# Pinning the block sums of feed-forward tile pairs in VectorE's program order

## The chip, the cores and the metric

The kernel runs on one core of one Trainium2 chip. The metric is the device time of one launch in microseconds (us). The core's engines run side by side, each through a queue of its own in a fixed order: TensorE (PE, with its weight loads shown as PEld), VectorE (DVE), ScalarE (ACT), GpSimd (POOL) and SyncE (SP), which here issues nearly all transfers between on-chip memory and DRAM. An engine that waits at an instruction holds up everything behind it in its queue.

## The reference

One layer of a transformer trunk on 1024 tokens with 1024 features: an attention mixer, then a feed-forward (SwiGLU), each with a modulated input and a layer norm on the way out. The change touches the feed-forward alone:

```python
def swiglu(h, w_in, w_out):                 # h 1024x1024, w_in 1024x5632, w_out 2816x1024
    gate, up = jnp.split(h @ w_in, 2, axis=-1)
    return (jax.nn.silu(gate) * up) @ w_out
...
x = layer_norm(DEEPNORM_ALPHA * x + gate2 * swiglu(h, ffn_w_in[i], ffn_w_out[i]), ln_g[i, 1], ln_b[i, 1])
```

All values are float32; the kernel splits each operand into a high and a low part and adds three products.

## The kernel before, in words

**The first products.** The hidden width of 2816 is cut into 22 feed-forward tiles of 128 (`ff`). For each, the products of the input with the gate and up weights are formed by a scheme of seven block products (a Strassen-Winograd form) rather than eight. They are the steps 1, 6, 2, 7, 5, 4, 3 of a tile, and a step is 12 matmuls (four blocks of the contraction by three partial products, lines 1073 to 1075). Steps 1 and 2 of the tiles 0 to 5 run ahead of the rest, so these tiles have five steps each (6, 7, 5, 4, 3: 60 matmuls); from tile 6 (`FIRST`) on all seven steps stand in a row (84 matmuls).

**The banks.** Steps 1 and 2 write PSUM banks `A`, of which there are two. Steps 6, 7 and 4 add up in one bank `B`, and steps 5 and 3 in one bank `D`, and there is one of each. After every step VectorE reads the bank as it then stands, and only when it has read it may the next step on that bank start: after step 6 line 1086 (`u2 = B + p1`), after 7 line 1088 (`u3 = B + p1`), after 5 line 1090 (`ub = D + u3`), after 4 line 1093 (`ua = B + p1`), after 3 line 1097 (`gb = D + u2`). TensorE can go on meanwhile with another bank. In tiles 0 to 5 step 7 follows step 6 on the same bank; the scheduler puts the first four or five matmuls of step 5 (bank `D`) between them as cover. From tile 6 on all of step 2 (bank `A`) lies there.

**The hidden tiles.** After step 3, ScalarE takes the silu of `gb` (line 1098) and GpSimd multiplies it in (`ub = ub * gb`, line 1099); `ua` has its own product on GpSimd after step 4 (line 1094). `u2` has one place in the tile `fd`, so that line 1086 of the next tile must stand behind line 1097 of this one. `ua` and `ub` have two places, for even and odd tiles.

**The block sums of a pair.** The second products, with `w_out`, use the same seven-product form, and want sums of the hidden blocks of two neighbouring tiles. `hidden_sums` makes them, four sums a pair, 11 pairs: `hs1 = ub + vb` (line 991), `hs2 = hs1 - ua` (992), `hs3 = ua - ub` (995), `hs4 = va - hs2` (996), where `ua`, `ub` are of the even tile and `va`, `vb` of the odd one. Each is stored to DRAM by SyncE (`store_hidden`, line 982). In the program's text the sums are written two steps after step 3 of the odd tile (lines 991 and 992) and one step later again (lines 995 and 996), through the list `late`.

**Other work beside it.** For each coming step one weight block is split: ScalarE casts the high part (line 844), VectorE subtracts for the low part (line 845); eight steps' blocks are held in `slots`. GpSimd makes the weight blocks' own sums (lines 828 to 831). The weight tiles `wi` are loaded two tiles ahead (line 804). Every ten steps `out_weights` makes sums of the `w_out` weights on VectorE (lines 1009 to 1013), already pinned.

**What sets the order.** The program is traced line by line and a scheduler then orders each engine's queue by its own estimate of when operands are ready; an instruction that it takes to be ready early moves ahead. `keep` is `tc.keep_in_program_order`: it ties an instruction behind the one that was traced just before it on the same engine. It adds no wait for another engine.

**After the first products.** The second products load their operands (`r`, lines 870 to 875) from the stored sums and the stored weights (`td`), split them as `ring` (lines 1029 and 1030), and multiply (lines 1222 to 1224). The two rows loaded at line 1143 reuse the memory of the block sums, so SyncE waits there for their stores.

Of the kernel before, what the change touches and what calls it, by code (L numbers as in the profile page):

```python
# [12 lines left out]
ALU = mybir.AluOpType  # L13
# [32 lines left out]
def fox_trunk_kernel(  # L46
# [17 lines left out]
    nc = tc.nc  # L64
# [911 lines left out]
    keep = tc.keep_in_program_order  # L976
# [4 lines left out]
    def store_hidden(ff, t, i):  # L981
        nc.sync.dma_start(sd[i][ff // 2], t)

    hs = {}

    def hidden_sums(ff, k, ua, ub, va, vb):

        if k == 0:
            hs.update({n: fp.tile([P, 512], F32, name=f"hs{n}_{ff}", tag=t, **({"bufs": 2} if t == "hb0" else {}))
                       for n, t in ((1, "a0"), (2, "a1"), (3, "hb0"), (4, "hb0"))})  # L990
            nc.vector.tensor_tensor(hs[1], ub, vb, ALU.add)
            nc.vector.tensor_tensor(hs[2], hs[1], ua, ALU.subtract)
            done = (5, hs[1]), (6, hs[2])
        else:
            nc.vector.tensor_tensor(hs[3], ua, ub, ALU.subtract)
            nc.vector.tensor_tensor(hs[4], va, hs[2], ALU.subtract)
            done = (7, hs[3]), (3, hs[4])
        for i, t in done:
            store_hidden(ff, t, i)
# [58 lines left out]
    def step(n):  # L1058
# [22 lines left out]
        if i == 1:  # L1081
            nc.scalar.copy(p1, b)
        elif i == 2:
            nc.scalar.activation(sa, b, AF.Silu)
        elif i == 6:
            nc.vector.tensor_tensor(u2, b, p1, ALU.add)  # L1086
        elif i == 7:
            nc.vector.tensor_tensor(u3, b, p1, ALU.add)
        elif i == 5:
            nc.vector.tensor_tensor(ub, b, u3, ALU.add)  # L1090
        elif i == 4:

            nc.vector.tensor_tensor(ua, b, p1, ALU.add)
            nc.gpsimd.tensor_tensor(ua, ua, sa, ALU.mult)
            late.append((n + 2, lambda: store_hidden(ff, ua, 1 + ff % 2)))
        else:
            nc.vector.tensor_tensor(gb, b, u2, ALU.add)
            nc.scalar.activation(gb, gb, AF.Silu)
            nc.gpsimd.tensor_tensor(ub, ub, gb, ALU.mult)
            if ff % 2:  # L1100
                late.append((n + 2, lambda: store_hidden(ff, ub, 4)))
                for k in range(2):
                    late.append((n + 2 + k + (ff + 1 >= FIRST), lambda k=k: hidden_sums(ff, k, fd[:, 4], fd[:, 2], fd[:, 5], fd[:, 3])))
# [200 lines left out]
```

## Time and profile before

| | us |
|---|---|
| median of 3 runs | 1428.95 (1426.27 to 1428.96) |
| profiled execution | 1424.15 |
| its span, first to last instruction | 1422.4 |
| PE busy | 1354.8 |
| DVE busy | 1011.5 |
| ACT busy | 585.2 |
| POOL busy | 340.1 |

The mean granted TensorE clock of the profiled execution is 0.989 of full speed. The first products run from about 762 to 1200 us of the span, the second ones from there to the end.

In the rows below a line of a timeline is: start in us, length in us, engine, source line, operation, tiles written and read, count; in brackets how long the engine had been idle and what released it. Lengths of one engine's instructions overlap a little, so the distance of starts is the better measure of a sequence. A line of the windows view is: stretch, its length, busy time (and instructions) of PE, PEld, DVE, ACT and POOL, the granted clock, the busy share of the transfer engines, GB/s. A line of the waits view is: who waited for whom, total us, times, longest.

### The profile page before, as it was taken

The page shows a single profiled execution, that of the slowest core. Times are in us where ns is not written, and L with a number is a line of the kernel's source. Part 1 is how long each engine was busy: PE and PEld are TensorE (multiplying, and loading weights), DVE is VectorE, ACT ScalarE, POOL GpSimd, SP SyncE. Part 2 cuts the span into 40 slices and gives each one's busy share as a digit, 9 for nine tenths or more (in the row PEclk, how much of TensorE's full clock was granted, in tenths as well). Part 3 has the DMA queues.
Part 4 walks back from the last instruction along what each step waited for, and adds up shares of the span by engine and source line. Part 5 has one row for each costly group of instructions (what it writes and reads, how often), then busy time and mean ns, then how long its engine had stood idle before and what let it go on. Part 6 is the DMA issues. An engine that isn't in the chain of part 4 may idle for free.

```text
span 1422.4 us, 19155 instructions
## 1 busy us (share of the span) xinstructions
PE 1354.8 (95%) x6832; PEld 1134.3 (80%) x6832; DVE 1011.5 (71%) x1636; ACT 585.2 (41%) x1025; POOL 340.1 (24%) x250
## 2 busy tenths in 40 slices
PE   5899999999999999999999889999999999899997
PEld 4677778887888888889997667888888888688886
DVE  6765586655988888888767655566666667685897
ACT  3532232123777776784236322333333334543320
POOL 2443003310111111132000444444444431000011
PEclk9999999999999999999999999999999999999999
DMA  9757775568655566527444332554655566996631
GB/s 274 202 175 235 245 215 182 186 192 213 143 130 138 135 151 151 137 82 258 165 147 137 96 119 95 195 175 158 199 191 167 181 205 228 348 296 225 193 119 74
DMA packets 212305, 254.41 MB, mean 179 GB/s; under 512 B 13353, under 2 KB 138609, under 8 KB 212210
## 3 DMA queue, kind: packets, MB, share of 16 engines
q1 hardware_dynamic: 211058, 251.09, 58.4%
q10 hardware_dynamic: 1152, 2.10, 0.4%
q8 instruction: 54, 0.88, 0.3%
q14 instruction: 41, 0.34, 0.1%
HBM read 185.18 MB, written 67.96 MB: 178 GB/s over the span
## 4 chain that ended last, share of the span: by engine, by line
PE 70%; DVE 12%; DMA 5%; POOL 5%; issue 4%; ACT 2%; SPq 1%; POOLq 0%; DVEq 0%; ACTq 0%
PE og L631 5%; PE y L1222 4%; PE y L1223 4%; PE y L1224 4%; PE B L1073 4%; PE t L596 4%; PE B L1075 4%; PE B L1074 4%; PE A L1073 3%; PE A L1074 3%; PE A L1075 3%; PE D L1075 3%; PE D L1074 2%; PE D L1073 2%; PE s L535 2%
## 5 line engine op out<-in xcount | busy, mean ns | idle before, releaser
L1222 PE MATMUL y<-ring 128*128 128x512 f32 (+1 forms) x319 | 122.7, 385 | 5.2 <-ACT fpu L1181 5.2
L1029 ACT CAST ring<-r 128x1024 fp32r<-128x1024 f32 x77 | 80.5, 1055 | 105.9 <-PE y L1224 59.1
L1030 DVE TENSOR_TENSOR ring<-r,ring 128x1024 fp32r<-128x1024 f32 x77 | 95.4, 1249 | 38.9 <-ACT ring L1029 31.0
L1223 PE MATMUL y<-ring 128*128 128x512 f32 (+1 forms) x319 | 122.6, 384 | 0.0
L1224 PE MATMUL y<-ring 128*128 128x512 f32 (+1 forms) x319 | 122.2, 384 | 0.0
L1073 PE MATMUL B<-XT,slots 128*128 128x512 f32 x264 | 105.0, 398 | 15.7 <-DVE fd L1086 12.7
L602 DVE TENSOR_TENSOR pl<-t,ph 128x512 fp32r<-128x512 f32 x192 | 103.9, 549 | 14.8 <-ACT ph L601 13.5
L844 ACT CAST slots<-wi 128x512 fp32r<-128x512 f32 x88 | 54.4, 623 | 141.7 <-PE D L1074 69.3
L543 ACT ACTIVATE p<-s,nm 128x640 f32<-128x640 f32 (+7 forms) x128 | 95.5, 746 | 39.1 <-DVE nm L542 38.7
L601 ACT CAST ph<-t 128x512 fp32r<-128x512 f32 x192 | 91.1, 480 | 44.3 <-PE t L596 41.8
L1074 PE MATMUL B<-XT,slots 128*128 128x512 f32 x264 | 103.7, 393 | 0.0
L1075 PE MATMUL B<-XT,slots 128*128 128x512 f32 x264 | 103.7, 393 | 0.0
L542 DVE TENSOR_REDUCE nm<-s 128x1 f32<-128x640 f32 (+7 forms) x128 | 95.6, 749 | 2.5
L596 PE MATMUL t<-ident,p 128*128 128x128 f32 x576 | 95.7, 273 | 0.6 <-DVE pl L602 0.4
L596 PEld LDWEIGHTS t<-ident,p 128*128 128x128 f32 x576 | 71.3, 141 | 11.5 <-DVE pl L602 2.2
L845 DVE TENSOR_TENSOR slots<-wi,slots 128x512 fp32r<-128x512 f32 x88 | 70.8, 804 | 9.8 <-ACT slots L844 9.8
L579 PE MATMUL o<-ph,va 128*128 128x512 f32 x192 | 76.5, 399 | 0.0
L1222 PEld LDWEIGHTS y<-ring 128*128 128x128 f32 x319 | 60.3, 189 | 18.5 <-ACT fpu L1181 5.6
L1073 PEld LDWEIGHTS B<-XT,slots 128*128 128x128 f32 x264 | 50.3, 191 | 29.2 <-DVE fd L1086 15.2
L535 PE MATMUL s<-ka,qa 128*128 128x320 f32 (+2 forms) x192 | 67.5, 352 | 5.0 <-ACT p L543 4.9
L1224 PEld LDWEIGHTS y<-ring 128*128 128x128 f32 x319 | 60.4, 189 | 11.8
L1223 PEld LDWEIGHTS y<-ring 128*128 128x128 f32 x319 | 60.4, 189 | 11.6
(571 smaller groups left out, 3747.1 us busy)
## 6 DMA issues: line engine op xcount, KB each, us to landing
wi<-in_ffn_w_in_dram SPq DMA_DIRECT2D x50, 512.0 KB
aw<-in_ada_w_dram SPq DMA_DIRECT2D x46, 512.0 KB
r<-sd SPq DMA_DIRECT2D x77, 256.0 KB
sd<-hs SPq DMA_DIRECT2D x44, 256.0 KB
r<-td SPq DMA_DIRECT2D x44, 256.0 KB
sd<-fd SPq DMA_DIRECT2D x33, 256.0 KB
r<-in_ffn_w_out_dram SPq DMA_DIRECT2D x33, 256.0 KB
qa<-qs SPq DMA_DIRECT2D x32, 256.0 KB
```

The costliest lines, as they stand in the source:

```text
L535: nc.tensor.matmul(o, qa[:, q], ka[:, c0:c0 + w], start=True, stop=False)
L542: nc.vector.tensor_reduce(nm, view, axis=axis, op=ALU.max, negate=True)
L543: nc.scalar.activation(pv, view, AF.Exp, bias=nm, accum_out=lcs[hf][:, s * 4 + jj:s * 4 + jj + 1])
L596: nc.tensor.transpose(tb[:, jj * P:(jj + 1) * P], probs[hf * 4 + jj][:, kbk * P:(kbk + 1) * P], ident)
L602: nc.vector.tensor_tensor(pl[:, c0:], tb[:, c0:], f32(ph[:, c0:]), ALU.subtract)
L1030: nc.vector.tensor_tensor(t[:, 1], raw, f32(t[:, 0]), ALU.subtract)
L1073: nc.tensor.matmul(b, hi, rh, start=(first and k == 0), stop=False, skip_group_check=True)
L1074: nc.tensor.matmul(b, hi, rl, start=False, stop=False, skip_group_check=True)
L1075: nc.tensor.matmul(b, lo, rh, start=False, stop=(k == 3), skip_group_check=True)
L1222: nc.tensor.matmul(b[:, c0:c1], sh, wh, start=first, stop=False, skip_group_check=True)
L1223: nc.tensor.matmul(b[:, c0:c1], sh, wl, start=False, stop=False, skip_group_check=True)
L1224: nc.tensor.matmul(b[:, c0:c1], sl, wh, start=False, stop=last, skip_group_check=True)
```

## The change

The four block sums are each wrapped in `keep`, and nothing else is altered:

```diff
         if k == 0:
...
-            nc.vector.tensor_tensor(hs[1], ub, vb, ALU.add)
-            nc.vector.tensor_tensor(hs[2], hs[1], ua, ALU.subtract)
+            keep(nc.vector.tensor_tensor(hs[1], ub, vb, ALU.add))
+            keep(nc.vector.tensor_tensor(hs[2], hs[1], ua, ALU.subtract))
             done = (5, hs[1]), (6, hs[2])
         else:
-            nc.vector.tensor_tensor(hs[3], ua, ub, ALU.subtract)
-            nc.vector.tensor_tensor(hs[4], va, hs[2], ALU.subtract)
+            keep(nc.vector.tensor_tensor(hs[3], ua, ub, ALU.subtract))
+            keep(nc.vector.tensor_tensor(hs[4], va, hs[2], ALU.subtract))
             done = (7, hs[3]), (3, hs[4])
```

The same instructions run on every engine; their order differs on VectorE and SyncE, a little on TensorE and ScalarE, and not on GpSimd. In the rows below `hs_1` are the sums of the pair of tiles 0 and 1 (the number at the end tells the four apart), `hs_7` of tiles 6 and 7, `hs_21` of 20 and 21; the numbers behind `B` and `D` tell the tiles apart.

VectorE where tile 0 ends and tile 1 begins, the difference:

```order
 L1097 TENSOR_TENSOR fd<-D_8666,fd 128x512
 L845 TENSOR_TENSOR slots<-sqb,slots 128x512
-L995 TENSOR_TENSOR hs_1_8840<-fd 128x512
 L1086 TENSOR_TENSOR fd<-B_8719,fc 128x512
 L845 TENSOR_TENSOR slots<-wi_12_8543,slots 128x512
```

`hs3` needs the even tile alone, and stood ahead of line 1086 of tile 1; it is gone from there. The same holds after tiles 2 and 4.

VectorE where tile 1 ends and tile 2 begins, before:

```order
L1097 TENSOR_TENSOR fd<-D_8755,fd 128x512
L845 TENSOR_TENSOR slots<-sqb,slots 128x512
L991 TENSOR_TENSOR hs_1_8838<-fd 128x512
L1086 TENSOR_TENSOR fd<-B_8808,fc 128x512
L845 TENSOR_TENSOR slots<-wi_14_8664,slots 128x512
L992 TENSOR_TENSOR hs_1_8839<-hs_1_8838,fd 128x512
L996 TENSOR_TENSOR hs_1_8841<-fd,hs_1_8839 128x512
L1088 TENSOR_TENSOR fd<-B_8808,fc 128x512
L845 TENSOR_TENSOR slots<-skb,slots 128x512
L1090 TENSOR_TENSOR fd<-D_8853,fd 128x512
```

and now:

```order
L1097 TENSOR_TENSOR fd<-D_8755,fd 128x512
L845 TENSOR_TENSOR slots<-sqb,slots 128x512
L1086 TENSOR_TENSOR fd<-B_8808,fc 128x512
L845 TENSOR_TENSOR slots<-wi_14_8664,slots 128x512
L991 TENSOR_TENSOR hs_1_8838<-fd 128x512
L992 TENSOR_TENSOR hs_1_8839<-hs_1_8838,fd 128x512
L1088 TENSOR_TENSOR fd<-B_8808,fc 128x512
L845 TENSOR_TENSOR slots<-skb,slots 128x512
L995 TENSOR_TENSOR hs_1_8840<-fd 128x512
L996 TENSOR_TENSOR hs_1_8841<-fd,hs_1_8839 128x512
L1090 TENSOR_TENSOR fd<-D_8853,fd 128x512
```

Line 1086 now stands ahead of all four sums; two of them stand ahead of line 1088 and two ahead of line 1090. The boundary after tile 3 reads the same.

VectorE after line 1086 of tile 8, where the sums of tiles 6 and 7 now meet the pinned sums of the `w_out` weights:

```order
L1086 TENSOR_TENSOR fd<-B_9470,fc 128x512
L845 TENSOR_TENSOR slots<-wi_25_9300,slots 128x512
L991 TENSOR_TENSOR hs_7_9499<-fd 128x512
L992 TENSOR_TENSOR hs_7_9500<-hs_7_9499,fd 128x512
L845 TENSOR_TENSOR slots<-sqb,slots 128x512
L1009 TENSOR_TENSOR gate1b<-gate1b 128x512
L1010 TENSOR_TENSOR gate1b<-gate2b,gate1b 128x512
L995 TENSOR_TENSOR hs_7_9501<-fd 128x512
L996 TENSOR_TENSOR hs_7_9502<-fd,hs_7_9500 128x512
L1088 TENSOR_TENSOR fd<-B_9470,fc 128x512
```

Before, all four stood ahead of line 1086 here. The sums of tiles 16 and 17 stand the same way; the other pairs from tile 4 on have no weight sums between lines 1086 and 1088, but for tiles 12 and 13, where they stand ahead of line 991.

SyncE, the stores of the last pair and the first loads behind them, before:

```order
L982 DMA sd_10_7028<-hs_21_11330 128x512
L982 DMA sd_10_7039<-hs_21_11331 128x512
L1237 DMA gate2b<-g2d 128x1024
L982 DMA sd_10_7006<-hs_21_11333 128x512
L870 DMA r_14_11377<-sd_3_7032 128x512
L875 DMA r_14_11377<-td_7054 128x512
L870 DMA r_15_11394<-sd_4_7033 128x512
L1143 DMA ln_11353<-in_ln_g_dram 128x1024
```

and now:

```order
L982 DMA sd_10_7028<-hs_21_11330 128x512
L982 DMA sd_10_7039<-hs_21_11331 128x512
L982 DMA sd_10_7050<-hs_21_11332 128x512
L982 DMA sd_10_7006<-hs_21_11333 128x512
L1237 DMA gate2b<-g2d 128x1024
L870 DMA r_14_11377<-sd_3_7032 128x512
L1143 DMA ln_11353<-in_ln_g_dram 128x1024
L1143 DMA ln_11355<-in_ln_b_dram 128x1024
L875 DMA r_14_11377<-td_7054 128x512
L870 DMA r_15_11394<-sd_4_7033 128x512
```

The store of `hs3` (sd_10_7050), which was issued some twenty rows earlier, is now among the last four, and two loads of `r` moved behind line 1143.

On TensorE step 5 lies around step 7: at each of the first four boundaries (into tiles 1 to 4) five of its matmuls stood ahead of step 7 and seven behind it, and now four and eight, as the boundary into tile 5 had it already.

## Rows read from the trace of the kernel before

**Rows 1.** The page, part 1: busy time, share, instructions of each engine.

```profile
PE 1354.8 (95%) x6832; PEld 1134.3 (80%) x6832; DVE 1011.5 (71%) x1636; ACT 585.2 (41%) x1025; POOL 340.1 (24%) x250
```

**Rows 2.** Windows view of a late stretch of the first products.

```profile
1150.00:1200.00 50.00, 50.00 (x222) 41.20 (x221) 33.67 (x44) 19.67 (x27) 12.29 (x9) 1.00 0.64 218
```

**Rows 3.** Waits view of PE, 760 to 1240 us.

```profile
PE B L1073 <- DVE fd L1086: 12.7, 6, 2.7
PE y L1222 <- ACT fpu L1181: 5.2, 1, 5.2
PE B L1073 <- DVE fd L1088: 3.0, 1, 3.0
```

**Rows 4.** Timeline of DVE, from tile 0 to tile 1 of the feed-forward.

```profile
808.27 0.69 DVE L1097 TENSOR_TENSOR fd<-D,fd 128x512 f32<-128x512 f32 x1 [1.43 <-PE D L1075]
...
812.43 1.73 DVE L995 TENSOR_TENSOR hs<-fd 128x512 f32<-128x512 f32 x1 [2.64 <-POOL fd L1099]
814.09 0.68 DVE L1086 TENSOR_TENSOR fd<-B,fc 128x512 f32<-128x512 f32 x1
814.69 1.15 DVE L845 TENSOR_TENSOR slots<-wi,slots 128x512 fp32r<-128x512 f32 x1
```

**Rows 5.** Timeline of POOL in the same stretch.

```profile
811.11 1.29 POOL L1099 TENSOR_TENSOR fd<-fd 128x512 f32<-128x512 f32 x1
812.35 1.26 POOL L830 TENSOR_TENSOR wi<-sqb,wi 128x512 f32<-128x512 f32 x1
```

**Rows 6.** Timeline of DVE: a step of tile 1, then tile 4 to 5.

```profile
820.89 0.69 DVE L1090 TENSOR_TENSOR fd<-D,fd 128x512 f32<-128x512 f32 x1 [0.31 <-PE D L1075]
...
823.61 0.69 DVE L1093 TENSOR_TENSOR fd<-B,fc 128x512 f32<-128x512 f32 x1 [1.43 <-PE B L1075]
...
877.55 0.69 DVE L1097 TENSOR_TENSOR fd<-D,fd 128x512 f32<-128x512 f32 x1 [1.43 <-PE D L1075]
...
880.32 0.69 DVE L995 TENSOR_TENSOR hs<-fd 128x512 f32<-128x512 f32 x1 [1.47 <-POOL fd L1099]
880.93 0.68 DVE L1086 TENSOR_TENSOR fd<-B,gate2b 128x512 f32<-128x512 f32 x1
...
891.97 0.69 DVE L1097 TENSOR_TENSOR fd<-D,fd 128x512 f32<-128x512 f32 x1 [0.97 <-PE D L1075]
```

**Rows 7.** Timeline of PE at the two boundaries of rows 4 and 6.

```profile
811.70 0.39 PE L1074 MATMUL D<-XT,slots 128*128 128x512 f32 x1
814.82 0.80 PE L1073 MATMUL B<-XT,slots 128*128 128x512 f32 x1 [2.73 <-DVE fd L1086]
...
880.75 0.39 PE L1073 MATMUL D<-XT,slots 128*128 128x512 f32 x1
881.67 0.50 PE L1073 MATMUL B<-XT,slots 128*128 128x512 f32 x1 [0.53 <-DVE fd L1086]
882.00 0.39 PE L1074 MATMUL B<-XT,slots 128*128 128x512 f32 x1
```

**Rows 8.** Windows view of two single microseconds of the first products.

```profile
816.00:817.00 1.00, 1.00 (x4) 0.81 (x3) 0.00 (x0) 0.00 (x0) 0.00 (x0) 0.50 0.26 47
...
867.00:868.00 1.00, 1.00 (x3) 0.73 (x3) 0.97 (x3) 0.00 (x0) 0.00 (x0) 0.50 0.04 12
```

**Rows 9.** Timeline of DVE, after tile 7 of the feed-forward.

```profile
938.70 0.70 DVE L845 TENSOR_TENSOR slots<-sqb,slots 128x512 fp32r<-128x512 f32 x1 [1.85 <-ACT slots L844]
...
941.61 0.68 DVE L1088 TENSOR_TENSOR fd<-B,fc 128x512 f32<-128x512 f32 x1
...
949.09 0.69 DVE L1097 TENSOR_TENSOR fd<-D,fd 128x512 f32<-128x512 f32 x1 [0.50 <-PE D L1075]
```

**Rows 10.** Timeline of DVE, block sums of the last pair.

```profile
1207.13 0.68 DVE L992 TENSOR_TENSOR hs<-hs,fd 128x512 f32<-128x512 f32 x1
...
1208.87 0.68 DVE L996 TENSOR_TENSOR hs<-fd,hs 128x512 f32<-128x512 f32 x1
```

**Rows 11.** Windows view of the load-bound stretch between first and second products.

```profile
1210.00:1215.00 5.00, 5.00 (x24) 4.14 (x23) 0.68 (x1) 0.00 (x0) 0.00 (x0) 1.00 0.90 273
```

## The prediction

> **What bounds the kernel now.** I read from the whole to the place. The page's first part has TensorE busy for 95% of the span and VectorE for 71% [rows 1], so an edit on VectorE is worth only what TensorE waits for it. In the first products from tile 6 on TensorE does not wait at all: 50.00 us busy in 50 us, 222 matmuls [rows 2]. The waits view of TensorE for the whole stage has three lines: 12.7 us for line 1086 in six waits, 3.0 us for line 1088 in one, and 5.2 us in one wait for a ScalarE copy, where the second products begin [rows 3]. The prize is in the first line. The place is the boundary from one tile to the next in tiles 0 to 5, seen in VectorE's timeline: line 1097 at 808.27, then a sum (line 995) which stands idle for 2.64 us and takes 1.73 us, and only then, at 814.09, line 1086 [rows 4]. The sum waits for GpSimd's product of line 1099, which ends at 811.11 + 1.29 = 812.40 [rows 5]. Line 1086 needs no part of it; it is only queued behind it.
>
> **What is lost there now.** Twelve matmuls take 2.72 us where nothing waits (line 1090 at 820.89 to line 1093 at 823.61) [rows 6], so one takes 0.227 and the 60 of a tile 13.60. From line 1097 of tile 0 at 808.27 [rows 4] to that of tile 5 at 891.97 [rows 6] there are five tiles in 83.70 us, where 5 x 13.60 = 68.00 would do: 15.70 us lost. The parts: at the first boundary the matmul after 811.70 could start at 811.93 and starts at 814.82, a gap of 2.89; the next matmul after a gap also comes 0.33 instead of 0.227 later (881.67 to 882.00), 0.10 more [rows 7]. Four boundaries are alike, 4 x 2.99 = 11.96. The fifth, from 877.55 to 891.97, loses 14.42 - 13.60 = 0.82 [rows 6]. That makes 12.78. [...]
>
> [...]
>
> **The change, part by part.** It adds no wait and no instruction. It moves 44 sums on VectorE with the SyncE stores that hang on them; GpSimd's queue stays as it is.
>
> *Line 1086 goes free.* At every boundary its earliest start is then step 6's end, 2.72 after line 1097: 880.27 at the fifth one, where it started at 880.93 behind a sum [rows 6]. TensorE follows 0.74 later (881.67 for 880.93), so at 881.01. The four matmuls of cover end with the one at 880.75, so the slot is 880.98 [rows 7]. That leaves 0.03 + 0.10 = 0.13 at each of five boundaries, since the first four now have four matmuls of cover too: **0.65 us stay**.
>
> *Two sums ahead of line 1088 (after tiles 1 and 3).* Counted from line 1097: line 1086 at 2.72, line 845 at 3.32, and if it takes 1.15 as in rows 4, line 991 at 4.47. Its GpSimd product is done at 812.40 - 808.27 = 4.13 [rows 4, 5], so the wait itself is hidden by lines 1086 and 845. Line 1088 must start by 7.22, so that step 4 has its slot at 3.43 + 20 x 0.227 = 7.96. No row shows the sums there; the neighbours are 0.69 [rows 6] and 1.73 [rows 4]. Two of 0.69 put line 1088 at 5.85, one of each at 6.89, two of 1.73 at 7.93, which is 0.71 + 0.10 too late, twice: 0 to 1.6. I take **0**, as one of each is still in time, and GpSimd's work of this kind ends soon after.
>
> The 1.73 stand beside GpSimd's line 830, which runs from 812.35 to 813.61 [rows 5]; the sum ends 0.55 after that, about its own 0.69. [...]
>
> *Two sums ahead of line 1090 (same places).* Line 1090 then starts at about 6.89 + 0.60 + 0.60 + 2 x 0.69 = 9.47; step 3 wants its bank at 7.96 + 2.72, so line 1090 may start as late as 9.94. Nothing is lost; this is the cover that is used up most.
>
> *Four sums ahead of line 1088 from tile 6 on.* There line 1088 may start 2 x 2.72 after line 1086, and since step 5 stands between, up to 7.22 after it without a wait. Six instructions at about 0.61 fit. Where the weight sums stand there too (pairs 6/7 and 16/17), lines 991 and 992 fall into VectorE's idle 1.85 us before 938.70, but lines 995 and 996 push line 1088 from 941.61 by 2 x 0.61 to 942.83. Line 1097 at 949.09 ran as soon as its bank was done [rows 9]; two steps before, 943.65, step 5 was done, the next step's slot is 0.20 before that (880.27 against 880.98 - 4 x 0.227 = 880.07 in rows 6, 7), and minus 0.74 the limit is 942.71. Late by 0.12 + 0.10, twice: **0.4 us lost**; none at best, and with one of the two sums at 1.73 some 2 x 1.34 = 2.7.
>
> *The last pair's stores.* TensorE already waits 5.2 us at the start of the second products [rows 3], for loads behind these stores in SyncE's queue. Before, line 996 starts 1.74 after line 992 (1207.13, 1208.87), with a split of `ring` between them; now line 995 is between, 2 x 0.60 = 1.20, so the last store is ready 0.54 earlier [rows 10]. But the store of `hs3`, 256 KB, comes into this stretch; at 273 GB/s with the transfer engines 0.90 busy [rows 11] it takes 0.96: 0.4 us net. Two loads of 256 KB moved behind line 1143's wait, up to 1.9 more. Ends: -0.5 if the store finds free time, 2.3 if nothing does. I count one of the two loads: **1.4 us lost**. The earlier pairs' stores move by some microseconds against weight loads that are two tiles ahead: nothing.
>
> **The sum.** 15.70 - 0.65 - 0 - 0.4 - 1.4 = 13.25 us. Nothing behind tile 5 waits for a clock of its own but the transfers above, so an earlier start is handed on to the end. The profiled execution took 1424.15 (span 1422.4 and 1.75 around it) and would take 1410.9. It was faster than all three timed runs; against their median of 1428.95 the sum gives **1415.7 us**.
>
> **The rivals.**
> (a) *The wait moves to line 1088.* If line 1099 comes later than in rows 5, line 991 waits as before and line 1088 is late in its place. That can be only after tiles 1 and 3: 2 x 2.99 come back, 13.25 - 6.0 = 7.3, **1421.7**. Against it speak the 0.34 us and the 1.37 of further cover (5.85 against 7.22).
> (b) *Given back at the second products.* If the loads there keep their time on the clock, the wait of 5.2 grows by all that was gained, and the kernel stays at **1428.9**. For it: the stretch is 0.90 busy with transfers [rows 11]. Against it: shortly before they are at 0.64 [rows 2], and most loads are issued when a buffer comes free, so they move along.
> (c) [...] If GpSimd runs beside the sums everywhere, each takes 1.73 and line 845 1.15. Then line 1088 starts 0.60 + 2 x 1.15 + 4 x 1.73 = 9.82 after line 1086 against 7.22: 2.60 + 0.10 for each of eight pairs (4/5 to 18/19) is 21.6, with 2.4 for the weight sums of two and 1.6 after tiles 1 and 3 it is 25.6; less the gain, 25.6 + 0.65 + 1.4 - 15.7 = 12.0 slower, **1440.9**. It decides at (7.22 - 0.60 - 2 x 0.69) / 4 = 1.31 us a sum. Against it: the sum of rows 6 takes 0.69. [...]
>
> **How the numbers follow.** Forecast 0.80, (a) 0.08, (b) 0.07, (c) 0.05. A measurement of this kernel can tell about 0.2%, 2.9 us, from no change. Faster: the forecast and (a), 0.88; within: (b), 0.07; slower: (c), 0.05. Range: at best 15.70 + 0.5, and two more slow-clock stretches saved in a usual run, 2.9, is 19.1: 1410. At worst 15.70 - 0.65 - 1.6 - 2.7 - 2.3, and one slow stretch left after the 3.0 us wait for line 1088, which the change does not touch, 1.46: 7.0, so 1422. (b) and (c) stay outside.
>
> **What would show it.** Right: the waits for line 1086 fall from 12.7 to under 2.5 us, of which 12.7 - 4 x 2.73 - 0.53 = 1.2 [rows 3, 7] belong to a wait inside tile 0 that stays; five tiles from line 1097 to line 1097 take 68 to 69 us; from tile 6 on TensorE stays at 50 in 50. Wrong: a new line for 1088 or 1090 in the waits of TensorE (a, c), or a wait for ScalarE's copy well above 6.6 (b).

## The result, and the profile after

The changed kernel takes **1408.83 us** (median of 4 runs, 1407.90 to 1410.20) against 1428.49 us (4 runs, 1426.27 to 1428.96) for the kernel before: a ratio of 0.9887, 95% interval 0.9860 to 0.9915. It is faster, as forecast, but by 19.7 us where 13.25 were predicted, and 1408.8 lies 1.2 us under the lower end of the range. The two profiled executions stand closer together: 1424.15 us before (span 1422.4) and 1409.46 us after (span 1407.7), 14.7 us apart. Compared again with more runs of the kernel before, the gain was 15.95 us (the second run of the changed kernel, below); the four runs of the kernel before here lie at the slow end of what it showed later, 1416.3 to 1428.3 us in 48 runs.

The waits view of TensorE covers the whole stage, 760 to 1240 us of the changed kernel (what waited, for whom; us in total, how often, the longest):

```profile
PE B L1073 <- DVE fd L1088: 4.8, 3, 3.1
PE y L1222 <- ACT fpu L1181: 2.8, 1, 2.8
PE B L1073 <- DVE fd L1086: 1.2, 1, 1.2
```

Against [rows 3], line 1086 has fallen from 12.7 us in six waits to the 1.2 us that belong to tile 0. Line 1088 has grown from one wait to three; the two new ones are 0.52 and 1.19 us. The wait at the start of the second products has fallen too, from 5.2 to 2.8 us, which I had not expected.

The starts of line 1097 in VectorE's timeline, one per tile, give the length of each tile (start, us, engine, line, operation; in brackets the idle time before it and who ended that):

```profile
808.02 0.69 DVE L1097 TENSOR_TENSOR fd<-D,fd 128x512 f32<-128x512 f32 x1 [1.43 <-PE D L1075]
...
821.80 0.69 DVE L1097 TENSOR_TENSOR fd<-D,fd 128x512 f32<-128x512 f32 x1 [1.43 <-PE D L1075]
...
836.36 0.69 DVE L1097 TENSOR_TENSOR fd<-D,fd 128x512 f32<-128x512 f32 x1 [1.43 <-PE D L1075]
```

Tile 1, from line 1097 of tile 0 to that of tile 1, takes 13.78 us and tile 2 takes 14.56. The next three, by the same line, take 13.78, 15.22 and 13.80; the five together 71.14 us instead of 83.70 [rows 4, 6]. The odd boundaries (after tiles 1 and 3) are the long ones. This is the first of them on VectorE:

```profile
824.52 0.69 DVE L1086 TENSOR_TENSOR fd<-B,fc 128x512 f32<-128x512 f32 x1 [1.20 <-PE B L1075]
825.12 1.35 DVE L845 TENSOR_TENSOR slots<-wi,slots 128x512 fp32r<-128x512 f32 x1
826.40 1.78 DVE L991 TENSOR_TENSOR hs<-fd 128x512 f32<-128x512 f32 x1
828.22 1.67 DVE L992 TENSOR_TENSOR hs<-hs,fd 128x512 f32<-128x512 f32 x1
829.81 0.68 DVE L1088 TENSOR_TENSOR fd<-B,fc 128x512 f32<-128x512 f32 x1
```

On GpSimd at that time, and then on TensorE:

```profile
825.88 1.75 POOL L830 TENSOR_TENSOR wi<-sqb,wi 128x512 f32<-128x512 f32 x1
827.71 1.62 POOL L831 TENSOR_TENSOR skb<-wi,wi 128x512 f32<-128x512 f32 x1
```

```profile
829.72 0.39 PE L1075 MATMUL D<-XT,slots 128*128 128x512 f32 x1
830.63 0.47 PE L1073 MATMUL B<-XT,slots 128*128 128x512 f32 x1 [0.52 <-DVE fd L1088]
```

Line 1086 is in time, 824.52, 2.72 us behind line 1097 as the prediction says. But both sums meet a GpSimd operation, line 830 and then line 831, and the two take 1.78 and 1.67 us instead of the 0.69 of [rows 6]. So line 1088 starts 8.01 us after line 1097, past the limit of 7.22, and TensorE's next matmul starts 0.91 after its predecessor instead of 0.23.

From tile 6 on TensorE does not wait, as before. The windows view of the changed kernel, columns as in [rows 2]:

```profile
900.00:950.00 50.00, 50.00 (x221) 41.13 (x220) 31.35 (x42) 15.49 (x27) 22.02 (x15) 1.00 0.52 174
1150.00:1200.00 50.00, 50.00 (x222) 41.20 (x221) 36.56 (x43) 19.84 (x24) 6.96 (x5) 1.00 0.75 253
```

VectorE has more to do there all the same. In the whole kernel it is busy for 1025.7 us, where it was 1011.5 with the same 1636 instructions, and 12.3 us of that lie between line 1097 of tile 0 and that of tile 21 (255.92 against 243.65). Of the eight sums of line 996 between tile 5 and the last pair, four now take 1.78 us, where all took 0.69 before. The one at 965.39, for example, stands beside line 829 of GpSimd (964.95 to 966.62).

The granted clock, the third column from the end of a line, does not fall again in the first products; before, it was 0.91 on the mean in two such stretches, which held those of [rows 8]. One stretch in tile 0 falls to 0.91. It follows the wait of 3.1 us in tile 0, which the change does not touch; in the profile before, the same 20 us, with a wait of 3.0, stood at 1.00:

```profile
790.00:810.00 20.00, 15.73 (x61) 12.19 (x61) 11.43 (x17) 4.42 (x8) 9.75 (x7) 0.91 0.31 93
810.00:830.00 20.00, 20.00 (x88) 15.86 (x86) 12.80 (x15) 5.01 (x8) 13.94 (x10) 1.00 0.28 79
...
850.00:870.00 20.00, 18.81 (x82) 14.85 (x81) 14.45 (x18) 5.58 (x9) 10.66 (x8) 1.00 0.44 145
```

The bookkeeping of the 14.7 us between the two profiles: 0.25 before tile 0 ends, 12.56 in the five tiles, 0.10 from tile 5 to tile 21, and 1.79 from line 1097 of tile 21 to the end (220.97 us before, 219.18 after).

### The profile page after: what moved, and what is told of

It is laid out like the page before. It is cut to its first block, busy times and chain, and to the rows that moved or that the text cites. A ratio compares the mean times of both kernels' runs of the same rounds, so it can differ in the third digit from the quotient of the medians.

```text
span 1407.7 us, 19137 instructions
## 1 busy us (share of the span) xinstructions
PE 1354.5 (96%) x6832; PEld 1133.2 (81%) x6832; DVE 1025.7 (73%) x1636; ACT 584.6 (42%) x1025; POOL 343.5 (24%) x250
## 4 chain that ended last, share of the span: by engine, by line
PE 71%; DVE 13%; DMA 5%; POOL 4%; issue 3%; ACT 2%; SPq 1%; POOLq 0%; DVEq 0%; ACTq 0%
PE og L631 5%; PE y L1222 4%; PE y L1224 4%; PE y L1223 4%; PE B L1073 4%; PE B L1074 4%; PE B L1075 4%; PE t L596 4%; PE A L1073 3%; PE A L1075 3%; PE A L1074 3%; PE D L1073 3%; PE D L1075 3%; PE D L1074 3%; PE s L535 2%
## 5 line engine op out<-in xcount | busy, mean ns | idle before, releaser
L596 PEld LDWEIGHTS t<-ident,p 128*128 128x128 f32 x576 | 71.2, 141 | 11.5 <-DVE pl L602 2.2
L1073 PE MATMUL A<-h2h,slots 128*128 128x512 f32 x176 | 69.1, 392 | 0.0
```

Source lines behind the costliest of these rows:

```text
L596: nc.tensor.transpose(tb[:, jj * P:(jj + 1) * P], probs[hf * 4 + jj][:, kbk * P:(kbk + 1) * P], ident)
L1073: nc.tensor.matmul(b, hi, rh, start=(first and k == 0), stop=False, skip_group_check=True)
```

## The experiments

Three questions were open: is it line 1086 alone that gave the five tiles back, and how much of the time is the granted clock's; what is left at the odd boundaries; and why the passage to the second products became shorter. The theories go by letters in what was expected. A: the gain is that of line 1086 at the tile boundaries. B: it is made at the passage to the second products. C: the rest, by which runs of one kernel differ, is the number of half-clock stretches (granted clock 0.50, [rows 8]). D: what is left at the odd boundaries is the two sums that run beside GpSimd ahead of line 1088. F, G and H are on the passage and are told there. "Five tiles" means from line 1097 of tile 0 to that of tile 5, "the end part" from line 1097 of tile 21 to the end of the span.

### The kernel before, once more

> The kernel before once more, unaltered, to see its timed executions with their granted clock. Theory C (slow clock): the timed runs of before (median 1428.5) are some 4 us slower than its profiled one (1424.15, clock 0.989) because the four gaps of 2.7 us of TensorE after tiles 0 to 3 are followed by a half-clock stretch (about 1.46 us each) in a number that differs from run to run; then times and mean clocks go together: runs near 1428 show a clock near 0.986 to 0.987, a run near 1424 shows 0.989. Rival: the difference has nothing to do with the clock; then runs near 1428 show 0.989 too. The five tiles take 83.7 us in the profile with two slow stretches, 82.2 with one, 86.6 with four.

Measured: 1424.31 us median (10 runs, 1416.62 to 1427.57), ratio 0.9996 (0.9980 to 1.0013) to the 23 runs of the kernel before in the same series, which lie between 1419.07 and 1428.28. The five tiles took 86.97 us in its profile, not 83.70: the tiles 18.20, 16.63, 19.50, 18.23 and 14.41. Two stretches of its windows view:

```profile
822.00:838.00 16.00, 13.27 (x59) 10.66 (x58) 9.92 (x13) 3.40 (x6) 7.63 (x6) 1.00 0.46 147
838.00:858.00 20.00, 17.27 (x64) 13.63 (x63) 8.86 (x12) 3.97 (x7) 8.76 (x8) 0.83 0.27 79
```

The same gap on TensorE, 2.73 us, is in both stretches. In the tile of the first one (16.63 us) the clock stays at 1.00; the next one (19.50 us) has it granted at 0.83 on the mean. If it falls to the 0.50 of [rows 8] there, that is some 7 of the 20 us, by my estimate. All 48 runs of this kernel in two series (33 here, 15 with the changed kernel below) follow their mean granted clock: the one at 0.995 took 1416.62 us, the three at 0.993 took 1416.3 to 1419.1, the five at 0.986 took 1424.3 to 1427.6. A straight line through them falls by 1.2 us for each 0.001, and the runs scatter by about 1.2 us around it. So the time of the kernel before is set in part by how many of its four equal gaps are followed by a half-clock stretch: two tiles are longer than 16.6 us in its first profile (18.06 and 17.96), three in this one. It is only a part. This profile's execution took 1422.51 us, less than the first one's 1424.15 in spite of the longer tiles, because tile 0 ended at 803.62 us and not at 808.27, with a mean clock up to there of 1.00 against 0.99. In the twelve profiles shown here the end of tile 0 lies between 803.6 and 809.4 us, and the change has no part in that.

### Only tiles 0 to 5, only the last pair

```
-            nc.vector.tensor_tensor(hs[1], ub, vb, ALU.add)
+            pin(nc.vector.tensor_tensor(hs[1], ub, vb, ALU.add))
...  (and so for hs[2], hs[3], hs[4])
+        pin = keep if ff < FIRST else (lambda i: i)       # the first of the two kernels
+        pin = keep if ff == NF - 1 else (lambda i: i)     # the second; NF is 22
```

> Only the sums of the pairs 0/1, 2/3 and 4/5 are pinned. Theory A (the gain is line 1086 set free in tiles 0 to 5): the five tiles take 71.1 us as in the changed kernel, the stretch from line 1097 of tile 21 to the end stays at 221.0 as before, and the time is about 1410 to 1412. Theory B (the gain comes from the last pair's stores and the loads behind them): five tiles 83.7, time about 1427.

Measured: 1410.53 us median (4 runs, 1408.73 to 1412.24), ratio 0.9905 (0.9886 to 0.9923). The five tiles took 71.04 us, line 1086 is waited for 1.2 us; the end part, 221.35 us, stayed that of the kernel before, with the copy of line 1181 28.18 us behind line 1097 of tile 21.

> Only the sums of the last pair 20/21 are pinned. Theory A: five tiles 83.7 us as before (80.8 to 86.6 by the number of slow-clock stretches), from line 1097 of tile 21 to the end 219.2 as in the changed kernel, time about 1.8 us under before, 1426 to 1427. Theory B: time near 1410.

Measured: 1422.36 us median (10 runs, 1416.15 to 1426.62), ratio 0.9996 (0.9980 to 1.0012), no difference that can be measured. The five tiles took 86.93 us as in the copy of the kernel before; the end part fell from 221.0 us in that profile to 220.2, not to the 219.2 expected, and the copy of line 1181 came 27.53 us behind line 1097 of tile 21, 0.7 us sooner (28.19).

So the twelve sums of the three pairs of tiles 0 to 5 carry the gain in the first stage. The last pair's four carry a small one at the end, which the profile shows and the time does not. The two are separate.

### Only the later two sums of each pair

The four sums stand in `pin` as above; only its condition is another.

```
+        pin = keep if k == 1 else (lambda i: i)
```

> The kernel before with only the later two sums of every pair (hs3 and hs4) kept in their written place; hs1 and hs2 stay free to move ahead. If each boundary is paid for by the sums that move ahead of L1086 there, and by nothing that is carried from one to the next, the tiles that end at the second half's places take 13.8 us and the others stay at 16.6 us (18.1 us where the clock is down to half after the wait): tiles 1, 3 and 5 short, tiles 2 and 4 long, the five tiles 74.6 to 77.6 us, and the time 6 to 10 us under the kernel before. If the loss is one of a shared queue (the first late tile makes the later ones late), then freeing one half would give much less or much more than half of 13 us.

Measured: 1413.08 us median (4 runs, 1410.56 to 1414.19), ratio 0.9917 (0.9899 to 0.9935), 11.3 us under the kernel before. The tiles took 13.78, 18.13, 13.81, 16.63 and 13.82 us, the five 76.17, which is in the span expected; the gain in time is over the 6 to 10 us expected; I had left out the end part, which fell from 221.0 to 219.0 us. In its waits view line 1086 stands thus:

```profile
PE B L1073 <- DVE fd L1086: 6.7, 3, 2.7
```

Of the six waits of [rows 3], three are left: tile 0's 1.2 and two of 2.7. Each boundary pays for its own sum, and only one of the two that still had a gap had a tile of 18.1 us.

### The sums behind line 1088

```
-                    late.append((n + 2 + k + (ff + 1 >= FIRST), ...
+                    late.append((n + 3 + (ff + 1 >= FIRST) * k, ...
```

> The changed kernel, but after tiles 1 and 3 lines 991 and 992 are written one step later, so that all four sums stand behind line 1088 and ahead of line 1090. Theory D (the 2.2 us that came back after tiles 1 and 3 are line 1088 behind two sums that run beside GpSimd): the tiles 2 and 4 take 13.8 us each in place of 14.56 and 15.22, the five tiles 69.0, and the time is about 2.2 us under the changed kernel, 1406.6. Rival: four sums ahead of line 1090 make that one late instead: the waits of TensorE then name line 1090 and the five tiles stay at 71 or more.

Measured: 1407.60 us median (6 runs, 1402.52 to 1410.57), ratio 0.9884 (0.9863 to 0.9904). The tiles took 13.77, 14.12, 13.82, 14.09 and 13.77 us, 69.57 together, not the 69.0 expected: 1.57 us under the changed kernel, and all of the difference lies at the odd boundaries. VectorE's timeline of this kernel behind tile 1:

```profile
825.10 0.69 DVE L1088 TENSOR_TENSOR fd<-B,fc 128x512 f32<-128x512 f32 x1 [1.86 <-PE B L1075]
...
826.31 0.69 DVE L991 TENSOR_TENSOR hs<-fd 128x512 f32<-128x512 f32 x1
827.03 0.69 DVE L992 TENSOR_TENSOR hs<-hs,fd 128x512 f32<-128x512 f32 x1
...
828.85 0.68 DVE L1090 TENSOR_TENSOR fd<-D,fd 128x512 f32<-128x512 f32 x1
```

Line 1088 starts 6.54 us after line 1097 (818.56) and waits for TensorE again, not TensorE for it. The same two sums take 0.69; line 831 is over by then, as line 845 reads its result, `skb`, at 825.71. What is left, about 0.33 us at each odd boundary, stands at line 1090, in front of which there are now four sums: the first matmul behind it starts at 829.67, 0.46 after its predecessor.

### Two sums behind line 1088, two behind line 1090

```
             keep(nc.vector.tensor_tensor(hs[1], ub, vb, ALU.add))
+            keep(nc.vector.tensor_tensor(hs[3], ua, ub, ALU.subtract))
+            done = (5, hs[1]), (7, hs[3])
+        else:
             keep(nc.vector.tensor_tensor(hs[2], hs[1], ua, ALU.subtract))
-            done = (5, hs[1]), (6, hs[2])
-        else:
-            keep(nc.vector.tensor_tensor(hs[3], ua, ub, ALU.subtract))
             keep(nc.vector.tensor_tensor(hs[4], va, hs[2], ALU.subtract))
-            done = (7, hs[3]), (3, hs[4])
+            done = (6, hs[2]), (3, hs[4])
...
-                    late.append((n + 2 + k + (ff + 1 >= FIRST), ...
+                    late.append((n + 3 + k, ...
```

> The changed kernel with the four sums dealt out anew: hs1 and hs3 (both need only ua and ub) are written together behind the D products' copies of L1088, and hs2 and hs4 together one step later, in every pair of tiles. If the lateness at the odd boundaries (0.96 and 1.62 us, of which putting both sums behind L1088 took away all but about 0.33) is that of every sum that stands ahead of L1088 or L1090 while GpSimd adds, then tiles 2 and 4 take 13.8 us like the others, the five tiles 68.9 us, and the kernel is 2.2 us under the changed one and 0.7 us under the variant with both sums behind L1088. If what is left there is something else (the rows of ScalarE or the loads), the five tiles stay at 69.6 us. If the sums now come so late that the stores of the last pair hold back the layer-norm loads L1143, the part from L1097 of tile 21 to the end grows over 219.2 us.

Measured: 1407.08 us median (4 runs, 1404.53 to 1410.25), ratio 0.9879 (0.9858 to 0.9899). The tiles took 13.77, 13.78, 13.81, 13.79 and 13.78 us, 68.93 together, the number expected; the end part was 218.65 us, so the later sums hold up nothing there. In the waits view line 1088 is back to one wait, the one of tile 0 that [rows 3] had already:

```profile
PE B L1073 <- DVE fd L1088: 3.0, 1, 3.0
PE y L1222 <- ACT fpu L1181: 2.5, 1, 2.5
PE B L1073 <- DVE fd L1086: 1.2, 1, 1.2
```

In the profile this is the shortest pair of stages of all kernels here, 2.2 and 0.5 us under the changed one. In time it cannot be told from it: the changed kernel, run in the same series, is the next entry.

> The changed kernel once more, unaltered, so that it stands on the same chip as the variants of it. Both theories of the run's spread agree here: five tiles 0 to 5 at about 71.1 us between the starts of L1097, and the difference to the kernel before between 13 us (if the kernel before runs with one slow-clock stretch or two, as in its first profile) and 18 us (if it runs with three or four, as in the profile of the copy). The wait of the ScalarE copy L1181 in the last part again at about 27.1 us behind L1097 of tile 21.

Measured: 1408.41 us median (5 runs, 1404.35 to 1410.19), ratio 0.9879 (0.9859 to 0.9898) to 1424.36 us (15 runs of the kernel before, 1416.33 to 1427.30). The five tiles took 70.87 us and the copy came 26.93 us behind line 1097. The gain here is 15.95 us, between the two I had named. At equal mean granted clock it is less: at 0.993 the kernel before took 1416.33 to 1419.07 us and the changed one 1408.41 and 1408.58; the fitted line above puts the five runs of the changed kernel 11.4 us under the kernel before. The median clock is 0.989 before and 0.993 after. So some 11 us go with the work itself, the gaps in the five tiles and the shorter end part, and the other 4 to 5 with the clock. That split is an estimate, since the mean clock is that of the whole kernel. The tiles bear it out: in the five profiles here that have all four gaps, the five tiles are 2.8, 6.0, 6.0, 2.8 and 6.0 us longer than the 80.94 that four tiles of 16.63 and one of 14.42 make, 4.7 us on the mean; in the profiles of the changed kernel no tile from 1 on has such an extra.

### The passage to the second products

What the change did there, beside VectorE's order, is in SyncE's order of the last pair, shown ahead of the prediction: the two layer-norm loads of line 1143 moved ahead of two loads into `r_14` and `r_15`, and the last store, that of `hs4`, moved ahead of line 1237. That line, which I had passed over, is a broadcast load of 512 KB:

```
    nc.sync.dma_start(gate2b, g2d.to_broadcast([P, D]))
```

The first experiment makes only the first of the two moves, in the kernel before:

```
+    raws2, lns, last_r, behind = {}, [], [], lambda on: tc.issue_after(lns[1].ins) if on else ExitStack()
...
-        nc.sync.dma_start(t[:, 0], sd[i][j])
+        with behind(14 < m < 20): last_r.append(nc.sync.dma_start(t[:, 0], sd[i][j]))
...
-            nc.sync.dma_start(t[:, 1], td[j][:, i in (4, 6), i in (6, 7)])
+            with behind(13 < m < 20): nc.sync.dma_start(t[:, 1], td[j][:, i in (4, 6), i in (6, 7)])
...
-            nc.sync.dma_start(t, src[0, k:k + 1].to_broadcast([P, D]))       # line 1143
+            lns.append(nc.sync.dma_start(t, src[0, k:k + 1].to_broadcast([P, D])))
...
-        nc.sync.dma_start(a, x1d[tt])
+        with tc.issue_after(last_r[-1].ins): nc.sync.dma_start(a, x1d[tt])
```

`m` counts the loads of `r`, so those of `r_14` to `r_19` are held behind line 1143, and the loads of `x1d` behind them.

> The kernel before, with VectorE's order as it was; only SyncE's order in the last pair is that of the changed kernel: the two layer-norm loads L1143 are issued ahead of the load of td into r_14 and that of sd into r_15. To be read in the profile, from L1097 of tile 21 on: if it is the loads beside the last stores that held these back (theory F: a store landed 4.21 us after its issue before, 2.2 us now), the copy L1181 starts 27.1 to 27.5 us behind L1097 and TensorE waits 2.8 to 3.5 us for it, as in the changed kernel, and the part to the end shrinks by 1 to 1.8 us from 221 us. If it is the sums' own earlier place (theory G), the copy stays at 28.2 to 28.6 us and the wait at 4.3 to 5.2 us. Tiles 0 to 5 stay as in the kernel before, 83.7 to 87 us by the clock granted. The measured time should be equal to before or up to 1.8 us below, which this spread may hide.

Measured: 1422.80 us median (10 runs, 1418.80 to 1426.02), ratio 0.9995 (0.9977 to 1.0014). SyncE's issues in its timeline, and line 996 of VectorE's:

```profile
1203.29 0.42 SPq L1237 DMA_DIRECT2D gate2b<-g2d  x1
1204.66 0.32 SPq L982 DMA_DIRECT2D sd<-hs  x1
1205.07 0.39 SPq L870 DMA_DIRECT2D r<-sd  x1
1208.92 0.33 SPq L1143 DMA_DIRECT2D ln<-in_ln_g_dram  x1
```

```profile
1203.95 0.68 DVE L996 TENSOR_TENSOR hs<-fd,hs 128x512 f32<-128x512 f32 x1
```

With the loads out of the way, line 1143 still comes 4.26 us after the store was issued, 4.29 after the sum ended (1204.63). In the kernel before it came 4.26 after the sum. SyncE's own waits view says what it waits for there, the store:

```profile
SPq L1143 <- DMA sd<-hs: 3.4, 1, 3.4
```

The copy stayed 28.78 us behind line 1097 and the wait at 4.0 us. My theory F falls. G, the sums' own 0.54 us, fits this run but not the others: the gap from the end of line 996 to line 1143 is 2.58 us in the changed kernel, 2.60 in its second run and 2.59 when only the last pair is pinned. What these have in common is the store ahead of line 1237. That is theory H, and it was tried in both directions. First the same kernel, with the store and the broadcast in the other order (the first load of `r_14` is held behind the store too, where it stood already):

```
-    nc.sync.dma_start(gate2b, g2d.to_broadcast([P, D]))
+    with tc.issue_after(stores[-1].ins): nc.sync.dma_start(gate2b, g2d.to_broadcast([P, D]))
```

> The kernel of sp_loads_moved_only with one swap more in SyncE's order: the last store of the last pair (hs4) stands ahead of the 512 KB broadcast load L1237 into gate2b, where it stood behind it; VectorE's order is that of the kernel before. Theory H: the store's bytes wait on the transfer engines behind the broadcast's, so it lands some 1.7 us later than it would; the layer-norm load L1143, which waits for it, then comes 2.2 to 2.7 us behind the end of L996 as in the changed kernel, not 4.3; the copy L1181 then starts 27.1 to 27.6 us behind L1097 of tile 21 (28.8 in sp_loads_moved_only; L996 is still 0.54 us later than in the changed kernel), and TensorE's wait for it is 2.4 to 3.5 us, not 4.0. Theory G (the sums' place on VectorE, 0.54 us, and nothing of the queue): L1143 stays 4.3 us behind the end of L996 and the copy at 28.2 to 28.8 us. Tiles 0 to 5 as in the kernel before.

```profile
1211.17 3.79 SPq L982 DMA_DIRECT2D sd<-hs  x3
1215.02 0.42 SPq L1237 DMA_DIRECT2D gate2b<-g2d  x1
1215.53 0.40 SPq L870 DMA_DIRECT2D r<-sd  x1
1216.87 0.33 SPq L1143 DMA_DIRECT2D ln<-in_ln_g_dram  x1
```

```profile
1213.94 0.68 DVE L996 TENSOR_TENSOR hs<-fd,hs 128x512 f32<-128x512 f32 x1
```

```profile
SPq L1143 <- DMA sd<-hs: 0.9, 1, 0.9
```

Line 1143 now comes 2.25 us behind the end of line 996 (1214.62), 2.04 us sooner than with the broadcast ahead. The wait for the store fell from 3.4 to 0.9 us. The copy moved from 28.78 to 27.08 us behind line 1097, and the matmul that waits for it from 29.41 to 27.71. TensorE's wait was 4.1 us all the same, not the 2.4 to 3.5 expected: it had also come to the place sooner. The end part fell only from 220.5 to 219.9 us, and the granted clock behind the wait was lower: 0.83 on the mean from 20 to 40 us behind line 1097, against 0.91. (One run, 1428.22 us at a mean clock of 0.985; the time of a single run tells nothing here.) Then the changed kernel with the broadcast put back ahead of the store:

```
-            store_hidden(ff, t, i)
+            (nc.sync.dma_start(gate2b, g2d.to_broadcast([P, D])) if (ff, i) == (21, 3) else None, store_hidden(ff, t, i))
```

> The changed kernel, VectorE's order unaltered, with the broadcast load L1237 put ahead of the last pair's last store again, as the kernel before has it (the scheduler then also puts the layer-norm loads L1143 behind the loads of r_14 and r_15 as it did there). Theory H: L1143 comes 4.0 to 4.3 us behind the end of L996 and the copy L1181 28.0 to 28.7 us behind L1097 of tile 21, TensorE's wait for it 4 to 5 us, so the part to the end is 1.2 to 1.8 us longer than the changed kernel's 219.2 us, and the kernel gives back that much. Theory G: 27.1 us and 219.2 us as in the changed kernel, L1143 at 2.6 us. Five tiles 0 to 5 at 71.1 us under both.

```profile
1197.93 0.45 SPq L999 DMA_DIRECT2D gate2b<-g2d  x1
1198.47 0.41 SPq L982 DMA_DIRECT2D sd<-hs  x1
...
1203.51 0.33 SPq L1143 DMA_DIRECT2D ln<-in_ln_g_dram  x1
```

```profile
PE y L1222 <- ACT fpu L1181: 5.8, 1, 5.8
```

Measured: 1414.37 us in one run. (The broadcast is line 999 in this kernel.) Line 996 ended at 1198.13, so line 1143 comes 5.38 us behind it, even more than the 4.0 to 4.3 expected; the copy is 29.14 us behind line 1097, and the end part 222.07 us, 2.9 us longer than in the changed kernel. The matmul that waits for the copy starts at 29.77 instead of 27.69 us, and the clock behind it is 0.83 instead of 0.91. The five tiles are 70.88 us. H holds both ways for the landing of the store, and here it is more than I had expected. The issue times fit that: in the five profiles with the broadcast ahead, line 1143 comes 5.6 to 5.9 us after the broadcast is issued, and here the broadcast was issued 0.54 us ahead of the store, where it was 1.37 in the kernel with the loads moved. My estimate from these times is that less of the broadcast was done when the store was issued; this kernel loses 1.1 us more than the kernel before. That was not tried by itself.

All twelve profiles sort by this one place. With the store ahead of the broadcast, line 1143 comes 9.8 to 10.4 us behind line 1097 of tile 21 and SyncE waits 0.8 to 1.2 us there for stores (seven profiles); with the broadcast ahead it comes 12.4 to 13.0 us behind, and the wait is 2.3 to 3.4 us (five). The matmul behind the copy starts at 27.3 to 28.2 us in the seven and at 28.8 to 29.8 in the five. The end part sorts in the same way, though not by much: 218.7 to 220.2 us in the seven, 220.5 to 222.1 in the five. The clock behind TensorE's wait, from 20 to 40 us behind line 1097, goes with the spread in each group: in the seven, five profiles at 0.91 take 218.7 to 219.2 us and two at 0.83 take 219.9 and 220.2 (the latter is the kernel with only the last pair pinned); in the five, the one at 0.91 takes 220.5 and the four at 0.83 take 221.0 to 222.1. So of the 1.8 us that the end part gave back in the first two profiles (0.83 before, 0.91 after), I put a part down to the store's place and the sums' own 0.5 us, and a part to the clock behind a shorter wait.

## Why the prediction was right, and where it was not

**What bounds the kernel, line 1086 goes free: right.** The wait went from 12.7 to 1.2 us, as said. Line 1086 starts 2.72 us after line 1097. The tiles behind even boundaries take 13.78 to 13.80 us; the residue is 0.18 to 0.20 where 0.13 was worked out. Pinning only tiles 0 to 5 gives the whole of it. Two of the signs that were named did not come out: the five tiles took 71.14 us and not 68 to 69, and line 1088 got two new waits, which had been named as a sign of being wrong. Both are the next term.

**Two sums ahead of line 1088: the term was mis-sized.** I gave bounds of 0 and 1.6 us and took 0, "as one of each is still in time". Both sums took the longer time, 1.78 and 1.67 us after tile 1; the odd boundaries lost 0.96 and 1.62 over 13.60 us, 2.2 us more than the residue, so even the upper bound was too low. After tile 1 line 1088 came 8.01 us behind line 1097, near the 7.93 worked out for two sums of 1.73; after tile 3 it came at 8.66. Two things are in that. GpSimd's next operation, line 831, followed line 830 with hardly a break, so the ground "GpSimd's work of this kind ends soon after" was wrong: [rows 5] stop at line 830, one instruction too early. And behind tile 3 line 991 also waited 1.18 us for line 1099, which ended 5.23 us after line 1097 and not 4.13, and this lateness came on top. Rival (a), a wait that moves to line 1088, so came in part: for the reason that it gives after tile 3 alone, through the longer sums after both, and with a third of its price (2.2 of 6.0 us). That the sums' place is the cause is shown by the two kernels in which they stand elsewhere: with both behind line 1088 1.57 us came back, with two behind line 1088 and two behind line 1090 all 2.2. Beside GpSimd the two took 1.78 and 1.67 us, against 0.69 for the same sums when they stand behind line 1088; what makes a sum longer there no run shows. The prediction had two sums of 1.73 as its upper bound, and went by the milder case.

**Two sums ahead of line 1090: right here.** There is no wait for line 1090 in the changed kernel. The word "the cover that is used up most" was borne out by the variant with four sums there: 0.33 us lost at each odd boundary.

**From tile 6 on: 0.4 us lost was not seen.** From line 1097 of tile 5 to that of tile 21 it took 309.46 us before and 309.36 after. But the same part took 309.08 in the second profile of the kernel before and 310.40 in that of the changed one, so 0.4 is below what the profiles can tell.

**The last pair's stores: wrong in sign.** Forecast 1.4 us lost, found 1.8 gained (2.0 between the two second profiles). The step that failed is the choice of what the last store runs against. I priced the store of `hs3` and two loads by the mean rate of [rows 11], as if every byte in the stretch cost the same. What decides is which transfer stands ahead of the last store, because line 1143 waits for that store to land: with the 512 KB of line 1237 ahead of it the wait was over about 2.0 us later (4.29 us behind the sum, not 2.25), and the loads behind it, moved away, gave nothing (4.26 and 4.29 us after the sum). The order of SyncE ahead of the prediction shows this line changing places with the store, and no term of the sum named it. The 0.54 us of the earlier sum were right: line 996 starts 6.92 us behind line 1097 of tile 21 instead of 7.44.

**From the profile to the median: the largest part of the miss.** The sum came to 1410.9 for the profiled execution, and that was 1409.46. The errors above nearly cancel: 2.5 us too much counted for the five tiles; 0.5 too little for the middle, 3.2 for the end and 0.25 for the front: 1.45 too little in all. I then added the same 13.25 to the median of 1428.95, 4.8 us above the profiled execution, as if those 4.8 us stayed in the changed kernel. They did not: its four runs have their median 0.6 us below its profile. 1.45 + 4.8 + 0.6 are the 6.9 us between 1415.7 and 1408.8.

Two things are in the 4.8 us, and the runs do not part them. The first is the sample: in 48 later runs the kernel before has its median at 1424.1 us, beside its profile's 1424.15, and none is as slow as 1428.95; measured in one series later, the gain is 15.95 us. Why the first runs were slower stays open, since their granted clock is not on record. The second is the clock. The half-clock stretches behind the four gaps added 2.8 us in the first profile and 6.0 in three others; in the changed kernel two gaps are left, of 0.52 and 1.19 us, and its profile shows no half-clock stretch behind them. That can be up to 3.2 of the 4.8 us. The range allowed 2.9 us for it, two stretches, as its best case, and some of it belonged in the forecast. No run shows its 1.46 us a stretch, which is half of 15.70 - 12.78. The two long tiles of the first profile took 18.06 and 17.96 us, 1.3 to 1.4 us more than the 16.63 of a tile in which the clock stays at 1.00; single microseconds of them stand at 0.50 [rows 8]. That a usual run has more such stretches was an estimate, and no row of the first profile shows it. The profiles now show that their number differs from run to run: two long tiles in the first, three in the copy, for one and the same program.

Rival (b) did not come: the copy's wait fell where (b) has it grow. Rival (c) came in its cause and not in its price: more of VectorE's sums from tile 6 on met GpSimd, four of the eight of line 996 at 1.78 us, but none made TensorE wait.

## What to carry to other kernels

Sums that only stood in the queue ahead of what the critical engine needs cost it the wait for their own operand here, and moving them behind took 11.5 of its 12.7 us of waits away; but count what runs on GpSimd at the new place, one instruction further than the rows end: two sums took 1.78 and 1.67 us there, not 0.69. When an edit moves stores, look at every transfer that changes its place beside a store someone waits for, the large broadcast above all (its place made 2.0 us here), and not at the bytes of the whole stretch. In some runs the gaps of 2.7 us on TensorE were followed by half-clock stretches (tiles of 18.0 to 19.5 us, not 16.6), and the changed kernel, with gaps of 0.52 and 1.19 us left there, showed none in its tiles 1 to 5. So forecast from an execution's own profile, say what its slower runs have that goes too, and take enough runs of the kernel before to know where its median lies: four runs here gave 19.7 us, fifteen gave 15.95.

## What the runs showed of the hardware

- One program on one core took 1416.3 to 1428.3 us in 48 runs, a spread of 0.8%, and the time goes with the mean granted clock (0.995 to 0.986), about 1.2 us for each 0.001. The gap of 2.7 us that comes before a tile is followed by a half-clock stretch in some executions (tiles of 18.0 to 19.5 us; granted clock 0.50 in [rows 8]) and not in others (16.6 us).
- A VectorE sum of two 128x512 tiles in f32 took 0.69 us alone and 1.67 to 1.78 us where it started while a GpSimd operation ran (13 block sums in the first two profiles), and two sums in a row met two such operations in a row.
- A store of 256 KB issued behind a 512 KB broadcast load on the same queue was seen as landed 4.26 us after its issue. Ahead of that load, the wait for it was over 2.25 us after the sum that it stores, where it was 4.29 us with the load first. Both are read from the issue of line 1143, which waits for the store. That the store's bytes stood behind the broadcast's on the transfer engines (theory H) is an inference from the 2.0 us between the two orders; no run here shows the single transfers.
